# A hybrid RWKV-7 and block-sparse attention trunk on one core: g multiplied in split form, a fused key factor, openings to ScalarE, and a new order of work

## The chip, the cores and the metric

The kernel runs on one core of a Trainium2 chip. A core has TensorE (matrix products, results into PSUM banks), VectorE (DVE in the profile), ScalarE (ACT), GpSimd (POOL) and SyncE (SP), which issues the DMAs of this kernel. Each engine works through its own instructions in the order in which the program lists them, and waits on semaphores for the others. The metric is the device time of one execution in microseconds (us); lower is better.

## The reference, cut to what matters

Two layers over 256 tokens of width 1024, in float32: an RWKV-7 time mixing, and an attention layer. The sequence of 256 is one block of the block-sparse attention, so the second layer is plain causal attention of 16 heads of 64.

```python
def rwkv7_time_mix(h, ...):                      # h = rms_norm(x)
    xx = shifted(h) - h
    r, wdn, k, v, adn, gp = [(h + xx * mu[i]) @ w_in[:, cols(i)] for i in range(6)]
    decay = exp(-exp(-softplus(-(w0 + tanh(wdn) @ w2)) - 0.5))
    a = sigmoid(a0 + adn @ a2)
    kk = normalised_per_head(k * k_k)
    k = k * (1.0 + (a - 1.0) * k_a)
    # per token: S = S*decay - (S kk) (kk*a) + v k ;  y = S r
    y = group_norm(y) * gn_w + gn_b + sum(r * k * r_k) * v
    return (y * silu(gp)) @ w_out

x = x + rwkv7_time_mix(rms_norm(x))
kb, vb = shared_kv(x)                            # rms_norm, w_kv, norm and rotary on k
x = x + (softmax(q k^T, causal) v * silu(gate)) @ w_out_b
```

## The kernel before

**Projections.** x is held as two row blocks of 128 tokens (`b`) and the width as 8 k-tiles of 128. Each projection of the first layer is made in two halves of 512 columns (`n`): k0, r0, r1, k1, v0, v1, g0, g1, in the order `ORDER_A`. A half needs four quarters of its weights, each of 256 rows (two k-tiles) by 512 columns and 512 KB, which `loads` (L462) fetches into one of three `raw` buffers. Its other operand is the mixed input z = h + xx * mu, transposed, made by `mixed_split` (L684) into one or two of four pairs `zhi`, `zlo`.

A product of float32 operands is made in one of two ways in `products` (L501). *Split*: weights and z are each parted into a rounded high part (ScalarE copy into the type fp32r) and a low rest (VectorE subtraction, `split`, L381); three fp32r passes, low by high, high by low and high by high, go into the same PSUM bank. *Whole*: one float32 product of the unsplit operands, which the profile records as two rows. `WHOLE` lists the projections that are made whole: v and g. The split quarters lie in three pairs `whi`, `wlo`. A whole quarter stays in its `raw` buffer until both row blocks have used it.

**Recurrence.** The delta rule is computed in four chunks of 64 tokens. For each half n of the heads: `forms` (L855) makes the scaled keys, `in_chunks` transposes them and makes the products within a chunk (T, G), `inverse` (L972) inverts triangular blocks with many small VectorE steps and 32-wide TensorE products, and `recurrence` (L1122) runs chunk after chunk: TensorE, a copy by VectorE, TensorE, a scaling by ScalarE and VectorE, TensorE, a multiplication by VectorE. `evac_v` (L1068) centres v over each head of 64 and puts it into the operands `UV`. `group_norm` follows each row block, then `dense2` the output projection, whose second half of k-tiles needs the group norm of n = 1.

**Second layer.** Eight halves in the order `ORDER_B`; k, q, v and the gate g with inputs split in the same way; then scores, softmax, values, and the last output projection.

**What sets the order.** The program isn't written down in the order in which it runs. `Weave` simulates the engines while the program is being made: each part of the work is a generator that yields its operations with a rank from `PR` (lower goes first), and `dispatch` gives each free engine the ready operation with the lowest rank, by estimated durations. The order that comes out is fixed then; on the chip each engine follows it. Projection products have rank 100, so TensorE takes them when nothing else is ready. `either(a, b)` and `vg` leave an operation open to two engines. The second is taken only where the first one's backlog is longer by `ALT`:

```python
if op.alt and o is op.alt and self.backlog(op, prio) + op.us < o.us + ALT:
    continue
```

`Weave` also keeps a model of TensorE's clock (`COLD`, `WINDOW`, `PHASE`, `BUSY`, `KEEP`), and `warm_up` puts products of zeros before the first real ones until the planner's time `WARM[1]`. Buffers (`zs`, `his`, `raws`, `u2`, `bank`, `accs`) are given out by the same simulation.

Nearly all VectorE, ScalarE and GpSimd operations are recorded at L259, matrix products at L354, transposes at L357, DMAs at L364, whichever part they belong to; so groups are told apart by the tile names.

Of the kernel before, what the change touches and what calls it, by code (L numbers as in the profile page):

```python
# [37 lines left out]
class Op:  # L38
# [3 lines left out]
    def __init__(self, eng, us, emit, alt=None, table=None, columns=0.0, banks=(), port=0.0):  # L42
        self.eng, self.us, self.emit, self.alt, self.table = eng, us, emit, alt, table
        self.columns, self.banks, self.port = columns, banks, port
# [34 lines left out]
class Weave:  # L79
# [4 lines left out]
    def __init__(self):  # L84
        self.now, self.seq, self.heap = 0.0, 0, []
        self.queue = {e: [] for e in ("PE", "V", "S", "G", "D")}
        self.until = dict.fromkeys(self.queue, 0.0)
        self.table, self.parts, self.banks, self.recent = None, 0, {}, deque()
        self.port, self.holder = {"V": 0.0, "G": 0.0}, "V"
        self.window, self.active, self.cold = PHASE, 0.0, True  # L90
# [76 lines left out]
    def dispatch(self):  # L167
        for eng in ("PE", *("GV" if self.holder == "V" else "VG"), "S", "D"):
            queue = self.queue[eng]
            while self.until[eng] <= self.now + 1e-9:  # L170
                best, cooling = None, eng == "PE" and self.cooling()
                for entry in queue:
                    prio, seq, ready, o, op, _ = entry
                    if ready > self.now + 1e-9 or any(self.others(eng, b) > self.now + 1e-9 for b in o.banks):
                        continue
                    if o.port and self.port["G" if eng == "V" else "V"] > self.now + 1e-9:
                        continue
                    if op.alt and o is op.alt and self.backlog(op, prio) + op.us < o.us + ALT:
                        continue
                    key = (prio + (SWITCH if o.table not in (None, self.table) else 0)  # L180
                           - (1000 if cooling and o.columns > 2000 * o.us else 0), seq)
                    if best is None or key < best[0]:
                        best = key, entry
# [25 lines left out]
    def array(self, op):  # L209
# [4 lines left out]
        us, left = 0.0, 1.0  # L214
# [89 lines left out]
def yoco(ctx, tc, consts, x, norm_a, mu_a, w_in_a, w0_a, w2_a, a0_a, a2_a, kk_a, ka_a, rk_a,  # L304
# [43 lines left out]
    def pe(*mms):  # L348

        return Op("PE", sum(m[0] for m in mms), lambda: [m[1]() for m in mms], columns=sum(m[2] for m in mms),  # L350
                  banks=set().union(*(m[3] for m in mms)))

    def mm(dst, l, r, us, **kw):
        return us, lambda: nc.tensor.matmul(dst, l, r, **kw), size(r) * (1 if l.dtype == F32R else 4) * l.shape[0] / P, banks(dst)  # L354

    def tr(dst, src, idt):
        return max(0.045, 0.1085 * src.shape[0] / P), lambda: nc.tensor.transpose(dst, src, idt), 256 * src.shape[0] / P, banks(dst)  # L357
# [8 lines left out]
    def either(a, b):  # L366
        a.alt = b
        return a

# [250 lines left out]
    def normed(b, q, r):  # L620
# [4 lines left out]
        yield V.tensor_scalar(xn, xb[q, b], r, None, op0=ALU.mult)  # L625
        pt = yield bank
        yield tr4(pt, xn)
        if q == 0:
            yield V.tensor_tensor(hT[q][:, :, b1], pt.rearrange("p (a t) -> p a t", t=P), bc(na_T[:, 0:4], P), op=ALU.mult)
        else:  # L630
            yield [S.activation(hT[q][:, i, b1], pt[:, i * P:(i + 1) * P], AF.Copy, scale=na_T[:, 4 + i:5 + i])
                   for i in range(4)]
# [187 lines left out]
    def prep_k(n):  # L820
        yield event(f"ka{n}")
        for b in range(NB):
# [4 lines left out]
            yield vg("tensor_scalar", f, ia[n, b], 1.0, None, op0=ALU.subtract)  # L827
            yield vg("tensor_tensor", f, f, kab[f"ka{n}"], op=ALU.mult)
# [26 lines left out]
    def forms(n, b):  # L855
# [6 lines left out]
        yield V.tensor_scalar(nrm, nrm, 1e-24, None, op0=ALU.max)  # L862
# [109 lines left out]
    def inverse(n):  # L972
# [36 lines left out]
        yield V.tensor_scalar(XF[:, :, 0:16], X, w_th[0], None, op0=ALU.mult)  # L1009
        yield V.tensor_scalar(XF[:, :, 16:32], X, w_th[1], None, op0=ALU.mult)  # L1010
# [57 lines left out]
    def evac_v(n):  # L1068
        def f(b, acc):
# [10 lines left out]
            yield V.tensor_scalar(mv, mv, -1.0 / 64, None, op0=ALU.mult)  # L1080
            m4 = mv.rearrange("p (j q) -> p j q", q=2).unsqueeze(3).to_broadcast([P, 4, 2, 64])
            for cc in range(2):
                rows = slice(cc * 64, cc * 64 + 64)
                yield [vg("tensor_tensor", uv[n, 2 * b + cc][64 - q * 64:128 - q * 64, q], v4(vt)[rows, :, q, :],
                          m4[rows, :, q, :], op=ALU.add) for q in range(2)]
# [474 lines left out]
    for n in range(2):  # L1560
# [12 lines left out]
LAT, SWITCH, ALT = 0.16, 0, 24.59  # L1573
OWN = {"PE": 0.0, "V": 0.13, "S": 0.115, "G": 0.096, "D": 0.0}

PR = {"raw1": 55.8, "raw2": 76.3, "w2x": 32.2, "first": -129.5, "k0": 58.9, "r0": 111.3, "k1": -127.3, "r1": -14,
# [5 lines left out]
      "soft": 88.3, "values": -76.2, "out": 43.6}  # L1582

ORDER_A = ("k0", "r0", "r1", "k1", "v0", "v1", "g0", "g1")
FIRST = [(0, 1), (0, 0), (1, 1), (2, 1), (1, 0), (2, 0), (3, 0), (3, 1)]
# [3 lines left out]
WHOLE = "vg"  # L1589
ORDER_B = ("v0", "q1", "k0", "q0", "g1", "k1", "g0", "v1")  # L1590
# [4 lines left out]
COLD, WINDOW, KEEP, WARM = 1.9, 3.4133, 1852, (1.1, 5.39)  # L1595
PHASE, BUSY = 3.31, (3200, 3200)

# [53 lines left out]
```

## Time and profile before

| | us |
|---|---|
| median of 3 runs | 363.77 |
| lowest and highest | 363.22, 366.38 |
| the profiled execution | 362.5 |
| its span, first to last instruction | 360.7 |

The three runs took 366.38, 363.77 and 363.22. The profile is that of one execution; its mean granted TensorE clock is 0.991 of full speed. In the profile, a busy digit is the busy share of one of 40 equal slices in tenths. A group's row reads: line, engine, operation, out<-in by tile names, shape, count, then busy us and mean ns of one, then the idle time of the engine just before it and what ended it. In the timeline a row has the start, the duration and the number of equal instructions that were merged into it. Matrix products are pipelined, so that durations overlap: their pace is read from one start to the next.

### The profile page before, as it was taken

The numbers are of one execution on the slowest core, as the hardware profiler recorded it, in microseconds if no ns is written. First come the engines' busy times: TensorE is split into PE (matmuls) and PEld (weight loads), VectorE is DVE, ScalarE is ACT, GpSimd is POOL, SyncE is SP. The second block draws the span as 40 slices with busy tenths as digits, with TensorE's granted clock in tenths as the row PEclk, the third lists the DMA queues.
The fourth block names the chain that finished last, engine by engine and source line by source line (L and its number), as shares of the span: only waits on it lengthen the run. The fifth ranks groups of instructions, "written<-read, shape, count | busy, mean of one in ns | idle before, by whom it ended". The sixth has DMA issues, their size and how long they took to land.

```text
span 360.7 us, 7464 instructions
## 1 busy us (share of the span) xinstructions
PE 347.2 (96%) x2946; PEld 253.3 (70%) x2946; DVE 293.7 (81%) x588; ACT 187.6 (52%) x366; POOL 48.7 (14%) x73
## 2 busy tenths in 40 slices
PE   6999999999997999989999999999999999999995
PEld 5965668776554555465557777788889879876784
DVE  3999897999998689977759989658587879888653
ACT  5488948441061231242355357554664777698630
POOL 1100140000400000110102431005253005000000
PEclk9899999999999999998999999999999999999999
DMA  7764485454632724231544462475555353334303
GB/s 201 245 222 144 118 259 167 129 146 147 186 110 89 197 66 116 62 92 19 219 134 160 129 228 67 142 232 200 177 178 175 118 175 119 118 120 159 128 3 116
DMA packets 30331, 52.40 MB, mean 145 GB/s; under 512 B 4492, under 2 KB 5844, under 8 KB 30296
## 3 DMA queue, kind: packets, MB, share of 16 engines
q1 hardware_dynamic: 30296, 51.93, 46.5%
q8 instruction: 23, 0.38, 0.4%
q14 instruction: 12, 0.10, 0.1%
HBM read 48.26 MB, written 1.05 MB: 137 GB/s over the span
## 4 chain that ended last, share of the span: by engine, by line
PE 68%; DVE 15%; DMA 6%; ACT 5%; issue 3%; SPq 2%; POOL 0%; DVEq 0%; ACTq 0%
PE acc L354 51%; PE ps L354 12%; PE ps L357 5%; DVE UV L259 2%; DVE wlo L259 2%; ACT whi L259 2%; DVE u L259 2%; SPq L364 2%; DMA tri<-in_consts_dram 2%; DMA raw<-in_w_in_a_dram 2%; DMA raw<-in_w_kv_dram 1%; DVE XF L259 1%; DMA x<-in_x_dram 1%; DVE zlo L259 1%; DVE vn L259 1%
## 5 line engine op out<-in xcount | busy, mean ns | idle before, releaser
L259 DVE TENSOR_TENSOR wlo<-raw,whi 128x1024 fp32r<-128x1024 f32 x62 | 75.5, 1221 | 24.3 <-ACT whi L259 24.1
L259 ACT ACTIVATE whi<-raw 128x1024 fp32r<-128x1024 f32 x62 | 65.4, 1059 | 47.2 <-PE acc L354 30.2
L354 PE MATMUL acc<-whi,z 128*128 128x512 f32 x128 | 39.7, 392 | 0.0
L354 PE MATMUL acc<-wlo,zhi 128*128 128x512 f32 x88 | 37.9, 431 | 0.9 <-DVE wlo L259 0.7
L354 PE MATMUL acc<-whi,zlo 128*128 128x512 f32 x88 | 34.6, 393 | 0.0
L354 PE MATMUL acc<-whi,zhi 128*128 128x512 f32 x88 | 34.5, 393 | 0.0
L354 PE MATMUL acc<-raw,zhi 128*128 128x512 f32 x64 | 32.8, 637 | 0.0
L354 PE MATMUL acc<-raw,zlo 128*128 128x512 f32 x64 | 32.0, 617 | 0.0
L354 PEld LDWEIGHTS acc<-whi,z 128*128 128x128 f32 x128 | 24.1, 188 | 4.8
L354 PE MATMUL acc<-wlo,z 128*128 128x512 f32 x64 | 26.1, 408 | 0.0
L354 PE MATMUL acc<-zb,whi 128*128 128x256 f32 x128 | 23.1, 281 | 0.0
L354 PEld LDWEIGHTS acc<-wlo,zhi 128*128 128x128 f32 x88 | 16.5, 188 | 6.3 <-DVE wlo L259 2.4
L354 PE MATMUL acc<-whi,zb 128*128 128x512 f32 x64 | 20.0, 394 | 0.0
L354 PE MATMUL acc<-whi,zf 128*128 128x512 f32 x64 | 19.8, 391 | 0.0
L354 PEld LDWEIGHTS acc<-zb,whi 128*128 128x128 f32 x128 | 19.6, 188 | 0.0
L354 PEld LDWEIGHTS acc<-whi,zhi 128*128 128x128 f32 x88 | 16.5, 188 | 3.7
L354 PEld LDWEIGHTS acc<-whi,zlo 128*128 128x128 f32 x88 | 16.6, 188 | 3.3 <-issue 0.5
L354 PE MATMUL acc<-zb,wlo 128*128 128x256 f32 x64 | 18.9, 295 | 0.0
L259 ACT ACTIVATE UV<-ps 64x256 f32<-64x256 f32 x8 | 3.0, 378 | 29.6 <-DVE UV L259 16.3
L259 POOL TENSOR_TENSOR nrm<-nrm,half 128x8 f32<-128x8 f32 x4 | 7.8, 1950 | 77.5 <-DVE nrm L259 77.5
L354 PEld LDWEIGHTS acc<-raw,zhi 128*128 128x128 f32 x64 | 11.5, 197 | 9.4 <-issue 8.7
L354 PEld LDWEIGHTS acc<-raw,zlo 128*128 128x128 f32 x64 | 10.8, 189 | 9.4 <-issue 8.4
(216 smaller groups left out, 727.2 us busy)
## 6 DMA issues: line engine op xcount, KB each, us to landing
raw<-in_w_in_a_dram SPq DMA_DIRECT2D x32, 512.0 KB
raw<-in_w_kv_dram SPq DMA_DIRECT2D x16, 512.0 KB
raw<-in_w_in_b_dram SPq DMA_DIRECT2D x16, 512.0 KB
raw<-in_w_out_a_dram SPq DMA_DIRECT2D x8, 512.0 KB
raw<-in_w_out_b_dram SPq DMA_DIRECT2D x8, 512.0 KB
x<-in_x_dram SPq DMA_DIRECT2D x8, 256.0 KB
out_dram<-x SPq DMA_DIRECT2D x8, 128.0 KB
sw<-eL SPq DMA_DIRECT2D x8, 126.0 KB
```

Source lines behind the costliest of these rows:

```text
L259: return Op(eng, us, lambda: getattr(obj, name)(*a, **k), table=table, banks=banks(*a, *k.values()), port=port(eng, name, us, a, k))
L354: return us, lambda: nc.tensor.matmul(dst, l, r, **kw), size(r) * (1 if l.dtype == F32R else 4) * l.shape[0] / P, banks(dst)
L357: return max(0.045, 0.1085 * src.shape[0] / P), lambda: nc.tensor.transpose(dst, src, idt), 256 * src.shape[0] / P, banks(dst)
L364: return Op("D", us, lambda: [nc.sync.dma_start(a, b) for a, b in pairs])
```

## The change

1. `WHOLE` goes from "vg" to "v". g is made in the split form: its z goes through `split`, in two pairs `zhi`, `zlo` where one did, and its eight weight quarters are split by ScalarE and VectorE into `whi`, `wlo`.
2. In `prep_k` the two steps (ia − 1), times k_a, become one fused VectorE instruction.
3. Several operations that were VectorE's alone get ScalarE as an alternative through `either`: the normalised input and its gain for q = 0 (`normed`), two scalings in `inverse`, the scaling of the mean and the centring of v in `evac_v` (as four ScalarE activations, made into one operation by the new `several`). The `max` of the key norm gets GpSimd as an alternative; the centring loses it.
4. The planner learns of small TensorE operations: `narrow` marks those with fewer than 128 rows or columns; a change between narrow and full costs `SWAP` = 0.1 us in its simulation, and an operation of the other kind ranks later by `STICK` = 19.2.
5. All ranks in `PR` and several constants are new, and so are the order of the second layer's projections and the last two entries of `FIRST`. Warm-up products run until 8.23 of the planner's time rather than 5.39.

```diff
-    def __init__(self, eng, us, emit, alt=None, table=None, columns=0.0, banks=(), port=0.0):
+    def __init__(self, eng, us, emit, alt=None, table=None, columns=0.0, banks=(), port=0.0, narrow=False):
...
-                    key = (prio + (SWITCH if o.table not in (None, self.table) else 0)
+                    key = (prio + (SWITCH if o.table not in (None, self.table) else STICK if eng == "PE" and o.narrow != self.narrow else 0)
...
-        us, left = 0.0, 1.0
+        us, left = 0.0 if op.narrow == self.narrow else SWAP, 1.0
+        self.narrow = op.narrow
...
+    def several(ops):
+
+        return Op(ops[0].eng, sum(o.us for o in ops), lambda: [o.emit() for o in ops], banks=set().union(*(o.banks for o in ops)),
+                  port=sum(o.port for o in ops))
...
-        yield V.tensor_scalar(xn, xb[q, b], r, None, op0=ALU.mult)
+        yield either(V.tensor_scalar(xn, xb[q, b], r, None, op0=ALU.mult), S.activation(xn, xb[q, b], AF.Copy, scale=r))
...
-            yield vg("tensor_scalar", f, ia[n, b], 1.0, None, op0=ALU.subtract)
-            yield vg("tensor_tensor", f, f, kab[f"ka{n}"], op=ALU.mult)
+            yield V.scalar_tensor_tensor(f, ia[n, b], -1.0, kab[f"ka{n}"], op0=ALU.add, op1=ALU.mult)
...
-        yield V.tensor_scalar(nrm, nrm, 1e-24, None, op0=ALU.max)
+        yield vg("tensor_scalar", nrm, nrm, 1e-24, None, op0=ALU.max)
...
-        yield V.tensor_scalar(XF[:, :, 0:16], X, w_th[0], None, op0=ALU.mult)
-        yield V.tensor_scalar(XF[:, :, 16:32], X, w_th[1], None, op0=ALU.mult)
+        yield [either(V.tensor_scalar(XF[:, :, i * 16:i * 16 + 16], X, w_th[i], None, op0=ALU.mult),
+                      S.activation(XF[:, :, i * 16:i * 16 + 16], X, AF.Copy, scale=w_th[i])) for i in range(2)]
...
-                yield [vg("tensor_tensor", uv[n, 2 * b + cc][64 - q * 64:128 - q * 64, q], v4(vt)[rows, :, q, :],
-                          m4[rows, :, q, :], op=ALU.add) for q in range(2)]
+                dst = [uv[n, 2 * b + cc][64 - q * 64:128 - q * 64, q] for q in range(2)]
+                yield [either(V.tensor_tensor(dst[q], v4(vt)[rows, :, q, :], m4[rows, :, q, :], op=ALU.add),
+                              several([S.activation(dst[q][:, j, :], v4(vt)[rows, j, q, :], AF.Identity,
+                                                    bias=mv[rows, 2 * j + q:2 * j + q + 1]) for j in range(4)]))
+                       for q in range(2)]
...
-LAT, SWITCH, ALT = 0.16, 0, 24.59
+LAT, SWITCH, ALT = 0.16, 1.0, 26.61
...
-FIRST = [(0, 1), (0, 0), (1, 1), (2, 1), (1, 0), (2, 0), (3, 0), (3, 1)]
+FIRST = [(0, 1), (0, 0), (1, 1), (2, 1), (1, 0), (2, 0), (3, 1), (3, 0)]
...
-WHOLE = "vg"
-ORDER_B = ("v0", "q1", "k0", "q0", "g1", "k1", "g0", "v1")
+WHOLE = "v"
+ORDER_B = ("q0", "q1", "v0", "k0", "g1", "k1", "g0", "v1")
...
-COLD, WINDOW, KEEP, WARM = 1.9, 3.4133, 1852, (1.1, 5.39)
+COLD, WINDOW, KEEP, WARM = 1.9, 3.4133, 1045, (1.1, 8.23)
...
+SWAP, STICK = 0.1, 19.2
```

Of the ranks, those that the text names: `w` (weight splits from the fifth quarter on) goes from 82.4 to 58.2, `rec0` and `rec1` from −130 and 0.3 to 29.4 and −23.9, `inv0` and `inv1` from −77.8 and −83.1 to −69.4 and −78.7, `zg` from −65.2 to 77.6.

More of the change, by code (lines that the diff above doesn't have):

```diff
@@ L38 @@
 class Op:
-    def __init__(self, eng, us, emit, alt=None, table=None, columns=0.0, banks=(), port=0.0):
+    def __init__(self, eng, us, emit, alt=None, table=None, columns=0.0, banks=(), port=0.0, narrow=False):
         self.eng, self.us, self.emit, self.alt, self.table = eng, us, emit, alt, table
-        self.columns, self.banks, self.port = columns, banks, port
+        self.columns, self.banks, self.port, self.narrow = columns, banks, port, narrow
 class Slots:
@@ L89, in __init__ @@
         self.port, self.holder = {"V": 0.0, "G": 0.0}, "V"
-        self.window, self.active, self.cold = PHASE, 0.0, True
+        self.window, self.active, self.cold, self.narrow = PHASE, 0.0, True, False
     def at(self, t, f):
@@ L350, in pe @@
         return Op("PE", sum(m[0] for m in mms), lambda: [m[1]() for m in mms], columns=sum(m[2] for m in mms),
-                  banks=set().union(*(m[3] for m in mms)))
+                  banks=set().union(*(m[3] for m in mms)), narrow=any(m[4] for m in mms))
     def mm(dst, l, r, us, **kw):
-        return us, lambda: nc.tensor.matmul(dst, l, r, **kw), size(r) * (1 if l.dtype == F32R else 4) * l.shape[0] / P, banks(dst)
+        return us, lambda: nc.tensor.matmul(dst, l, r, **kw), size(r) * (1 if l.dtype == F32R else 4) * l.shape[0] / P, banks(dst), min(l.shape[0], size(l)) < P
     def tr(dst, src, idt):
-        return max(0.045, 0.1085 * src.shape[0] / P), lambda: nc.tensor.transpose(dst, src, idt), 256 * src.shape[0] / P, banks(dst)
+        return max(0.045, 0.1085 * src.shape[0] / P), lambda: nc.tensor.transpose(dst, src, idt), 256 * src.shape[0] / P, banks(dst), src.shape[0] < P
     def tr4(pt, src):
@@ L628, in normed @@
         if q == 0:
-            yield V.tensor_tensor(hT[q][:, :, b1], pt.rearrange("p (a t) -> p a t", t=P), bc(na_T[:, 0:4], P), op=ALU.mult)
+            yield either(V.tensor_tensor(hT[q][:, :, b1], pt.rearrange("p (a t) -> p a t", t=P), bc(na_T[:, 0:4], P), op=ALU.mult),
+                         several([S.activation(hT[q][:, i, b1], pt[:, i * P:(i + 1) * P], AF.Copy, scale=na_T[:, i:i + 1])
+                                  for i in range(4)]))
         else:
@@ L1079, in f @@
             yield V.tensor_reduce(out=mv, in_=heads(vt), op=ALU.add, axis=AX.X)
-            yield V.tensor_scalar(mv, mv, -1.0 / 64, None, op0=ALU.mult)
+            yield either(V.tensor_scalar(mv, mv, -1.0 / 64, None, op0=ALU.mult), S.activation(mv, mv, AF.Copy, scale=-1.0 / 64))
             m4 = mv.rearrange("p (j q) -> p j q", q=2).unsqueeze(3).to_broadcast([P, 4, 2, 64])
@@ L1569, in yoco @@
     weave.run()
-LAT, SWITCH, ALT = 0.16, 0, 24.59
+LAT, SWITCH, ALT = 0.16, 1.0, 26.61
 OWN = {"PE": 0.0, "V": 0.13, "S": 0.115, "G": 0.096, "D": 0.0}
-PR = {"raw1": 55.8, "raw2": 76.3, "w2x": 32.2, "first": -129.5, "k0": 58.9, "r0": 111.3, "k1": -127.3, "r1": -14,
[5 rows of a table removed]
-      "soft": 88.3, "values": -76.2, "out": 43.6}
+PR = {"raw1": 78.4, "raw2": 2.3, "w2x": 63.5, "first": -69.4, "k0": 122.5, "r0": 101.8, "k1": 90.1, "r1": 33.6,
[5 rows of a table added]
+      "values": 50.6, "out": -114.3}
 ORDER_A = ("k0", "r0", "r1", "k1", "v0", "v1", "g0", "g1")
-FIRST = [(0, 1), (0, 0), (1, 1), (2, 1), (1, 0), (2, 0), (3, 0), (3, 1)]
+FIRST = [(0, 1), (0, 0), (1, 1), (2, 1), (1, 0), (2, 0), (3, 1), (3, 0)]
 FIRST_B = [(0, 0), (1, 0), (2, 0), (0, 1), (1, 1), (2, 1), (3, 1), (3, 0)]
 SINGLE = "k"
-WHOLE = "vg"
-ORDER_B = ("v0", "q1", "k0", "q0", "g1", "k1", "g0", "v1")
+WHOLE = "v"
+ORDER_B = ("q0", "q1", "v0", "k0", "g1", "k1", "g0", "v1")
 N_U2, N_RAW = 4, 3
 URGENT = (1, 0)
-COLD, WINDOW, KEEP, WARM = 1.9, 3.4133, 1852, (1.1, 5.39)
+COLD, WINDOW, KEEP, WARM = 1.9, 3.4133, 1045, (1.1, 8.23)
 PHASE, BUSY = 3.31, (3200, 3200)
+SWAP, STICK = 0.1, 19.2
 def _constants():
```

10 rows, old and new, of the table PR are left out of this document.

## The prediction, made before the changed kernel was run

> **What bounds the kernel now.** I read the page first: the span, the engine totals, the slices of DVE and TensorE, and the shares of the chain that ended last.
>
> ```profile
> span 360.7 us, 7464 instructions
> PE 347.2 (96%) x2946; PEld 253.3 (70%) x2946; DVE 293.7 (81%) x588; ACT 187.6 (52%) x366; POOL 48.7 (14%) x73
> PE   6999999999997999989999999999999999999995
> DVE  3999897999998689977759989658587879888653
> PE 68%; DVE 15%; DMA 6%; ACT 5%; issue 3%; SPq 2%; POOL 0%; DVEq 0%; ACTq 0%
> ```
>
> TensorE is busy 96% of the span and carries 68% of the chain; no slice after the first shows it below 7 tenths, but for the last. VectorE is the second resource: nine tenths in a dozen slices, and 15% of the chain. ScalarE has half of its time free. So work taken from TensorE can shorten the kernel, but only where VectorE does not step into its place. The table by stage says where that could be. Columns: stretch, its length, busy time of TensorE, weight loads, VectorE, ScalarE and GpSimd, then the granted clock, DMA share and GB/s.
>
> ```profile
> 9.40:13.00 3.60, 3.60 (x18) 3.60 (x19) 3.60 (x8) 1.48 (x2) 0.84 (x3) 0.54 0.81 268
> 20.00:40.00 20.00, 19.89 (x69) 12.48 (x69) 17.94 (x35) 17.92 (x29) 0.00 (x0) 1.00 0.47 149
> 40.00:60.00 20.00, 18.37 (x112) 13.85 (x113) 18.50 (x32) 14.91 (x37) 4.90 (x4) 1.00 0.66 197
> 84.00:204.00 120.00, 116.19 (x1647) 68.94 (x1646) 101.76 (x206) 39.25 (x83) 12.62 (x14) 0.99 0.41 121
> 162.80:166.40 3.60, 3.60 (x8) 1.13 (x4) 3.47 (x6) 0.38 (x1) 0.00 (x0) 0.53 0.00 0
> ```
>
> From 84 to 204 us the two inverses, the two recurrences and the v and g projections run together. VectorE has 120 − 101.8 = 18.2 us free there, ScalarE 80.
>
> **The change, part by part.** The sum is made against the profiled execution, 362.5 us (span 360.7); the median of the runs is 363.8, and I carry the difference over at the end.
>
> *g split instead of whole (TensorE).* The four rows stand around the border between the last split projection and the first whole one.
>
> ```profile
> 84.09 0.39 PE L354 MATMUL acc<-wlo,zhi 128*128 128x512 f32 x1
> 85.45 0.39 PE L354 MATMUL acc<-wlo,zhi 128*128 128x512 f32 x1
> ...
> 86.81 7.03 PE L354 MATMUL acc<-raw,zhi 128*128 128x512 f32 x16
> 93.68 0.59 PE L354 MATMUL acc<-raw,zlo 128*128 128x512 f32 x1
> ```
>
> Six split passes go from 84.09 to 85.45, 0.227 us each from start to start, so a product of three passes takes 0.68. Sixteen rows of the whole form go from 86.81 to 93.68, 0.429 each, and a product is two rows, 0.86. (The 0.39 and 0.59 in the rows are durations with the pipelined tail; starts are what counts.) g has 2 halves × 2 row blocks × 8 k-tiles = 32 products: 32 × 0.86 = 27.5 becomes 32 × 0.68 = 21.8. **Term: −5.7**, all on the bounding engine.
>
> *g split instead of whole (VectorE, ScalarE).* Eight weight quarters and four z pieces must now be split.
>
> ```profile
> L259 DVE TENSOR_TENSOR wlo<-raw,whi 128x1024 fp32r<-128x1024 f32 x62 | 75.5, 1221 | 24.3 <-ACT whi L259 24.1
> L259 DVE TENSOR_TENSOR zlo<-u,zhi 128x512 fp32r<-128x512 f32 x4 | 2.7, 686 | 0.1
> L259 DVE TENSOR_SCALAR k<-ia 128x512 f32<-128x512 f32 x4 | 1.7, 422 | 0.1
> L259 DVE SCALAR_TENSOR_TENSOR k<-k,acc 128x512 f32<-128x512 f32 x4 | 2.7, 676 | 0.0
> L259 ACT ACTIVATE whi<-raw 128x1024 fp32r<-128x1024 f32 x62 | 65.4, 1059 | 47.2 <-PE acc L354 30.2 <-DMA raw<-in_w_in_a_dram 5.4 <-DMA raw<-in_w_out_a_dram 4.3
> L259 ACT ACTIVATE zhi<-u 128x512 fp32r<-128x512 f32 x4 | 2.5, 623 | 0.0
> ```
>
> VectorE gains 8 × 1.22 + 4 × 0.69 = 12.5 us, ScalarE 8 × 1.06 + 4 × 0.62 = 11.0. Both fit into the 18.2 and 80 us free, VectorE's with 5.7 to spare. No DMA is added: the eight quarters are fetched by the same SyncE issues, and a raw buffer now comes free after its split, not after its products. What this costs TensorE is a wait for a late `wlo`. The nearest rows are the 20 to 60 us stage, where sixteen quarters are split for k and r with VectorE as busy: TensorE idled 40 − 38.3 = 1.7 us there in all, 0.11 a quarter. Eight quarters: **+0.9**; bounds 0 (all hidden) and 12.5 (none).
>
> *One step of the key factor.* Four subtractions of 0.42 go; the multiply that stays takes the fused form, 0.68 as in the row of k from acc, as long as before. VectorE −1.7, at about 28 to 36 us, where TensorE loses 0.1 us in 20: hidden, **0**, bounds −1.7 and 0. The `max` of the norm stays on VectorE unless its queue is long; 0.
>
> *Openings to ScalarE.* The planner takes an alternative only where the backlog of the first engine exceeds the alternative by ALT (24.59, now 26.61 us), a queue that rows of half a microsecond hardly build. The rows bear it out: operations that already had an alternative never used it.
>
> ```profile
> L259 DVE COPY Z<-ZX 32x512 f32<-32x512 f32 x8 | 3.3, 417 | 0.1
> L259 DVE TENSOR_SCALAR bv<-bv,rsum 128x256 f32<-128x256 f32 x12 | 4.2, 347 | 0.0
> L259 DVE TENSOR_TENSOR UV<-vn,mv 64x256 f32<-64x256 f32 x16 | 6.7, 420 | 0.3
> L259 DVE TENSOR_SCALAR XF<-xw,con 128x256 f32<-128x256 f32 x4 | 1.3, 350 | 0.0
> L259 DVE TENSOR_SCALAR xn<-x,rs 128x512 f32<-128x512 f32 x4 | 1.8, 482 | 0.0
> ```
>
> All 8 spreads of Z ran on VectorE with ScalarE open to them, and so did the softmax scalings. So the centring of v (16, 6.7 us), the scalings of XF and xn (1.3, 1.8) stay where they are: **0**, with −9.8 of VectorE time as the bound if they all go.
>
> *Longer warm-up (5.39 to 8.23).* It adds dummy matmuls ahead of the first low-rank products.
>
> ```profile
> 9.38 3.61 PE L354 MATMUL ps<-hT,wl 128*128 128x128 f32 x16 [1.65 <-DMA wl<-in_w_in_a_dram]
> 12.83 0.60 PE L357 MATMUL ps<-con,xn 128*128 128x128 f32 x4
> ...
> 16.49 1.06 PE L354 MATMUL ps<-hT,wl 128*128 128x128 f32 x8
> 17.39 1.95 PE L354 MATMUL ps<-xxT,wm 128*128 128x128 f32 x16
> ```
>
> The first 16 took 3.45 us at a granted clock of 0.54 (first row of the table by stage); eight of the same later took 0.90, so 16 take 1.8. TensorE idled 1.65 us before them; dummies there would keep the clock. Up to −1.7. VectorE was busy in all 3.6 us of that stretch, so part comes back as waits for `xxT` and z: **−1.0**, bounds −1.7 and 0. Beside it: the Trainium skill, "TensorE: Matmul & The Clock Gate", Part 1, has the clock halve after an idle window of about 3.4 us and return after a busy one. The trace agrees with the halving and its length (3.6 us at 0.54). By that rule alone this term would be the full −1.7.
>
> *The end of the recurrence.* The second half of the output projection needs the group norm that follows the last chunk. Last `zlo` of each row block, and the first product that reads it:
>
> ```profile
> 202.85 0.69 DVE L259 TENSOR_TENSOR zlo<-ps,zhi 128x512 fp32r<-128x512 f32 x1
> 210.05 0.68 DVE L259 TENSOR_TENSOR zlo<-ps,zhi 128x512 fp32r<-128x512 f32 x1
> ...
> 206.68 0.39 PE L354 MATMUL acc<-zlo,zhi 128*128 128x512 f32 x1
> 213.28 0.40 PE L354 MATMUL acc<-zlo,zhi 128*128 128x512 f32 x1
> ```
>
> Ready at 203.5 and 210.7, read at 206.7 and 213.3: a slack of 3.1 and 2.6 us. A cover that shrinks by 5.7 against a chain that does not move exposes 5.7 − 2.6 = 3.1 us of idle TensorE. The chain does move: its steps wait behind products of 0.68 in place of 0.86, and with less cover it waits for less. Between 0 and 3.1 I take **+1.4**, near the middle.
>
> *The new order.* Labels and buffers change everywhere. Among the later projections only the first four change places; attention half 0 still has all four behind it, half 1 its keys after the sixth and its values after the eighth. g takes two z pairs, not one, and the second comes free only when k is through; that is well ahead of g. FIRST exchanges its last two entries. What another order does to the half-speed stretch at 162.8 (3.6 us at 0.53, 1.7 us lost) is open: **0**, bounds −1.7 and +1.7.
>
> Sum: −5.7 + 0.9 − 1.0 + 1.4 = −4.4, 362.5 to 358.1; on the median 363.8 to **359.4**.
>
> **The rivals.**
>
> *The chain holds.* If inverse and recurrence keep their length and the front gives nothing, only the slack is won: 363.8 − 2.6 = 361.2. For it: the chain is a ping-pong between engines, and 12.5 us more VectorE work stand beside it. Against: TensorE had hardly an idle slice there, so the chain was waiting for TensorE too.
>
> *VectorE's new work lands on the chain (slower).* Its place is 112 to 204 us. A subtraction of 1.22 us, once begun, is not interrupted, and every copy, scaling and multiply of inverse and recurrence that becomes ready meanwhile stands behind it; TensorE then runs dry before the group norm. If all eight stand in the chain it ends 9.8 us later; less the slack of 2.6 and the front's 1.0 that is +6.2: 370. It makes the kernel slower by over 3.6 us once more than 7.2 us, six of the eight, are met. For it: after the change VectorE would hold about 114 of 120 us. Against: the weight splits have a late rank (58.2) against the chain's (29.4, −23.9, −69.4, −78.7).
>
> *Fewer switches between small and full matmuls.* The planner now charges 0.1 us for one.
>
> ```profile
> 106.84 1.29 PE L354 MATMUL ps<-ZX,AB 16*32 16x32 f32 x128
> ...
> 126.12 1.98 PE L354 MATMUL acc<-raw,zlo 128*128 128x512 f32 x4
> 128.03 1.14 PE L354 MATMUL ps<-ZX,QS 32*32 32x32 f32 x60
> ...
> 199.33 0.69 PE L354 MATMUL ps<-UV,RR 128*64 128x64 f32 x16
> ```
>
> Four whole rows between two small blocks hold TensorE from 126.12 to 128.03, 1.91 where 4 × 0.429 = 1.72 would do: 0.19 a visit. From 106.84 to 199.33 I count 32 visits in the timeline. Half of them joined would give −3.0: 356.4. Against: a small part already ranks before every projection product (rank 100) with 19.2 added, so the new rule moves only small parts against transposes. Beside it: the Trainium skill, "TensorEngine Tiling (Array Packing)", Key Properties, says that a change of tiling mode drains the array; the trace agrees, with these 0.19 us.
>
> *ScalarE takes its openings after all.* VectorE then gains only 12.5 − 1.7 − 9.8 = 1.0 us, and the terms +0.9 and +1.4 go: 363.8 − 6.7 = 357.1.
>
> **How the numbers follow.** The forecast 0.38, switches 0.07, openings 0.05, the chain holds 0.30, VectorE slower 0.20. The runs shown lie within 363.2 to 366.4, so about 1% (3.6 us) is what a measurement can tell from no change. Faster by over 1% are the forecast and the two that go further, 0.50; within 1% the held chain, 0.30; slower 0.20. Likeliest 359.4, its own range 357 to 360. The wider range goes down past the joined switches with the full front and the half-speed stretch gone (356.4 − 0.7 − 1.7 = 354) and up to 368, inside the slower case: about one in ten left out on either side.
>
> **What would show it.** Right: half as many whole products (`raw`) as before, `wlo` 70 and no idle of TensorE over 1 us between 112 and 210; centring and XF still on VectorE; hT·wl 16 rows in about 1.8 us; the second-half products of the output projection start 4 to 6 us earlier than 206.7. The held chain: those products at 203 to 205 behind an idle TensorE. The slower case: VectorE above 9 tenths from 112 to 204, TensorE waiting for `wlo`, `u` or `UV`, and a granted clock below 1.0 in those stretches. What would make the sum wrong is above all the +1.4, taken between its bounds without a row that shows it.

## The result, and the profile after

| | before | after |
|---|---|---|
| median | 365.38 us (363.22 to 367.88, 20 runs) | 361.49 us (357.71 to 365.17, 20 runs) |
| ratio after to before | | 0.985, 95% interval 0.982 to 0.988 |
| profiled execution | 362.5 us, span 360.7, granted clock 0.991 | 362.5 us, span 360.7, granted clock 0.980 |

The ratio leaves out seven of the changed kernel's 20 runs, those more than 1.5% slower than its fastest; over all runs the medians stand at 0.989. The kernel is faster by 1.5%, or by 1.1% between the medians. The time lies inside the range and 2.1 us above the predicted 359.4. Of these 2.1 us, 1.6 come from the base: the forecast went from 363.8, the median of three runs, and 20 runs of the same kernel give 365.38. The change itself is −3.9 us between the medians, where the sum had −4.4. The two profiled executions happen to take the same time, and yet they are not the same: where one won, the other lost again.

The page of the changed kernel, engine totals, three rows of the slices, the shares of the chain:

```profile
PE 345.5 (96%) x2988; PEld 264.4 (73%) x2988; DVE 303.0 (84%) x596; ACT 201.0 (56%) x380; POOL 47.0 (13%) x73
PE   7999999999989999889999999999999999999995
DVE  2999889999999899997689989787457789999743
PEclk9999999999999999996599999999999999999999
PE 65%; DVE 26%; DMA 3%; issue 3%; ACT 2%; SPq 1%; POOL 0%; DVEq 0%; ACTq 0%
```

VectorE has 9.3 us more work than before, and its share of the chain went from 15% to 26%. The row of the granted clock dips to 6 and 5 tenths in two slices, near 170 us. The groups of instructions:

```profile
L355 PE MATMUL acc<-raw,zhi 128*128 128x512 f32 x32 | 14.9, 599 | 0.0
L355 PE MATMUL acc<-raw,zlo 128*128 128x512 f32 x32 | 14.9, 602 | 0.0
L260 DVE TENSOR_TENSOR wlo<-raw,whi 128x1024 fp32r<-128x1024 f32 x70 | 85.3, 1222 | 22.9 <-ACT whi L260 22.7
L260 DVE TENSOR_TENSOR UV<-vn,mv 64x256 f32<-64x256 f32 x16 | 6.7, 419 | 0.3
L260 DVE TENSOR_SCALAR xn<-x,rs 128x512 f32<-128x512 f32 x4 | 1.8, 483 | 0.0
L260 DVE SCALAR_TENSOR_TENSOR k<-ia,bv 128x512 f32<-128x512 f32 x4 | 2.8, 688 | 0.0
```

Half as many whole products, eight more low parts, the fused step in four instructions. All sixteen additions that centre v and the scalings of xn are still on VectorE: the openings to ScalarE were not used. Three places of the timeline: the first low-rank products, the first whole product, and the first product of the output projection's second half.

```profile
9.37 2.02 PE L355 MATMUL ps<-hT,wl 128*128 128x128 f32 x16 [0.62 <-DVE xxT L260]
...
85.76 6.60 PE L355 MATMUL acc<-raw,zhi 128*128 128x512 f32 x15
...
208.40 0.39 PE L355 MATMUL acc<-zlo,zhi 128*128 128x512 f32 x1
```

They were at 86.81 and 206.68 before. The front is 1.05 us shorter; but the middle took 122.64 us where it had taken 119.87, and only the second layer (152.3 us to the end, from 154.0) brings the total back. What TensorE waited for between 84 and 205 us (engine, line, releaser: us in total, times, longest):

```profile
PE ps L355 <- DVE UV L260: 1.8, 2, 1.0
PE ps L358 <- DVE sw L260: 1.4, 1, 1.4
PE ps L355 <- DVE u L260: 0.6, 1, 0.6
```

VectorE is named in all three. (The one for `sw` ends at 101 us, before the recurrence.) The longest of the first row is found in VectorE's timeline. The scaled operand `UV` is made in two halves, and between them stands a product of the second half's inverse, 1.00 us long:

```profile
149.48 0.42 DVE L260 TENSOR_TENSOR UV<-ps,eLT 64x256 f32<-64x256 f32 x1
149.82 1.00 DVE L260 TENSOR_TENSOR tmp<-xw 128x512 f32<-128x512 f32 x1
150.85 0.43 DVE L260 TENSOR_TENSOR UV<-ps,eLT 64x256 f32<-64x256 f32 x1
```

TensorE began its products at 150.04 and stood still for 0.99 us until the second half was there:

```profile
150.04 0.30 PE L355 MATMUL ps<-UV,WL 128*64 128x64 f32 x2
151.33 0.68 PE L355 MATMUL ps<-UV,WL 128*64 128x64 f32 x14 [0.99 <-DVE UV L260]
```

Then comes the loss. The table by stretches (columns as in the prediction) for the 15 us of such spells and the 14 us after them:

```profile
150.00:165.00 15.00, 11.46 (x371) 8.78 (x371) 14.13 (x24) 4.81 (x8) 3.66 (x3) 1.00 0.07 21
165.00:179.00 14.00, 14.00 (x213) 11.03 (x208) 9.21 (x16) 4.60 (x8) 0.00 (x0) 0.51 0.29 83
```

TensorE was busy for 11.5 of 15 us (13.5 before), and then ran 14 us at a granted clock of 0.51. It looks fully busy there because everything takes twice as long. The half-speed stretch of before was 3.6 us at 0.53.

### The profile page after: what moved, and what is told of

Read it like the earlier page. It is cut to its first block, busy times and chain, and to the rows that moved or that the text cites. A ratio compares the mean times of both kernels' runs of the same rounds, so it can differ in the third digit from the quotient of the medians.

```text
span 360.7 us, 7573 instructions
## 1 busy us (share of the span) xinstructions
PE 345.5 (96%) x2988; PEld 264.4 (73%) x2988; DVE 303.0 (84%) x596; ACT 201.0 (56%) x380; POOL 47.0 (13%) x73
## 3 DMA queue, kind: packets, MB, share of 16 engines
HBM read 48.26 MB, written 1.05 MB: 137 GB/s over the span
## 4 chain that ended last, share of the span: by engine, by line
PE 65%; DVE 26%; DMA 3%; issue 3%; ACT 2%; SPq 1%; POOL 0%; DVEq 0%; ACTq 0%
PE acc L355 45%; PE ps L355 15%; PE ps L358 5%; DVE wlo L260 4%; DVE XF L260 3%; DVE u L260 3%; DMA sw<-eL 2%; DVE tmp L260 2%; DVE UV L260 2%; DVE zlo L260 2%; DVE xw L260 1%; DVE RR L260 1%; DVE k L260 1%; DVE WL L260 1%; DMA vrow<-in_mu_a_dram 1%
## 5 line engine op out<-in xcount | busy, mean ns | idle before, releaser
L260 DVE TENSOR_TENSOR wlo<-raw,whi 128x1024 fp32r<-128x1024 f32 x70 | 85.3, 1222 | 22.9 <-ACT whi L260 22.7
L260 ACT ACTIVATE whi<-raw 128x1024 fp32r<-128x1024 f32 x70 | 74.0, 1060 | 46.0 <-PE acc L355 37.1
L355 PE MATMUL acc<-wlo,zhi 128*128 128x512 f32 x120 | 53.1, 442 | 0.5 <-ACT zhi L260 0.4
L355 PE MATMUL acc<-whi,zlo 128*128 128x512 f32 x120 | 47.9, 399 | 0.2 <-DVE zlo L260 0.2
L355 PE MATMUL acc<-whi,zhi 128*128 128x512 f32 x120 | 47.8, 398 | 0.0
L355 PEld LDWEIGHTS acc<-whi,zhi 128*128 128x128 f32 x120 | 23.0, 192 | 5.3
L260 ACT ACTIVATE zhi<-u 128x256 fp32r<-128x256 f32 (+1 forms) x16 | 8.2, 531 | 12.6 <-DVE u L260 12.6
L355 PE MATMUL acc<-raw,zhi 128*128 128x512 f32 x32 | 14.9, 599 | 0.0
L355 PE MATMUL acc<-raw,zlo 128*128 128x512 f32 x32 | 14.9, 602 | 0.0
L355 PEld LDWEIGHTS acc<-wlo,z 128*128 128x128 f32 x64 | 12.0, 188 | 2.8 <-issue 0.5
```

Of the source, the lines that this page charges most:

```text
L260: return Op(eng, us, lambda: getattr(obj, name)(*a, **k), table=table, banks=banks(*a, *k.values()), port=port(eng, name, us, a, k))
```

## The experiments

"Middle" is the stretch from the first whole product to the output projection's first second-half product, in the one profiled execution of each; the clock is the range over all its runs.

| run | median us (runs) | ratio to before, 95% | middle us | granted clock |
|---|---|---|---|---|
| changed, second sample | 358.54 (4) | 0.984, 0.972 to 0.996 | 119.30 | 0.980 to 1.000 |
| changed, g whole | 367.54 (10) | 1.002, 0.997 to 1.008 | 121.41 | 0.980 to 1.000 |
| before, g split | 380.74 (4) | 1.045, 1.033 to 1.057 | 131.03 | 0.958 to 0.967 |
| g's low parts on ScalarE | 358.60 (4) | 0.981, 0.961 to 1.000 | 117.32 | 0.979 to 1.000 |
| g's low parts made twice | 369.26 (10) | 1.009, 1.005 to 1.012 | 129.96 | 0.976 to 1.000 |
| g's low parts on GpSimd | 366.86 (10) | 0.998, 0.994 to 1.001 | 126.75 | 0.966 to 0.986 |
| warm-up of ten products | 360.26 (4) | 0.985, 0.980 to 0.991 | 118.80 | 0.967 to 1.000 |
| zero passes in the gaps | 359.32 (6) | 0.979, 0.976 to 0.981 | 120.10 | 0.995 to 1.000 |
| key factor in two steps | 359.58 (4) | 0.982, 0.978 to 0.986 | 118.85 | 0.993 to 1.000 |
| second half's v centred by ScalarE | 356.92 (4) | 0.974, 0.970 to 0.978 | 115.25 | 0.995 to 1.000 |
| the same, order of the change | 360.75 (6) | 0.986, 0.980 to 0.992 | 120.48 | 0.976 to 0.999 |
| all v centred by ScalarE | 360.19 (4) | 0.982, 0.977 to 0.987 | 115.67 | 0.995 to 1.000 |

**The changed kernel once more.** No edit.

> The changed kernel unaltered, for a second profile. Theory A (the clock): the shorter products leave TensorE idle spells between 149 and 164 us, and in some executions its clock then falls to half for up to four stretches; time and granted clock go together, about 0.36 us for each 0.001 of mean clock, from 356 us of span at 1.000. Then this profile lies on that line, and the less clock it lost between 160 and 180 us, the shorter it is by half of the time lost. Theory B (the chain): the time is set by the recurrence whatever the clock; then two profiles with different clocks have the same span within 1 us.

Its profiled execution kept full clock: 359.1 us, span 357.3. The same two stretches and the same landmarks:

```profile
150.00:165.00 15.00, 11.08 (x359) 8.35 (x359) 13.87 (x23) 4.98 (x8) 3.67 (x3) 1.00 0.06 20
165.00:179.00 14.00, 13.24 (x279) 9.97 (x279) 12.88 (x21) 6.03 (x10) 1.84 (x2) 1.00 0.36 116
```

```profile
85.74 6.60 PE L355 MATMUL acc<-raw,zhi 128*128 128x512 f32 x15
...
205.04 0.39 PE L355 MATMUL acc<-zlo,zhi 128*128 128x512 f32 x1
```

279 matrix products in 165 to 179 us where the other execution made 213: the 3.4 us between the two (208.40 − 205.04) are the clock. The idle spells before are the same in both, so they do not bring the fall each time. Over all 24 runs of the changed kernel the nine with a clock of 0.999 or above take 358.4 us on average, the four at 0.980 take 362.9 and the four at 0.971 take 364.1. (The kernel before is no steadier: in the 54 runs of it that were made beside the experiments its clock lies between 0.976 and 0.995, 0.987 on average, and the changed kernel's average is 0.988.)

**Split of g alone, both ways.**

```diff
-WHOLE = "v"
+WHOLE = "vg"    # in the changed kernel; the reverse in the kernel before
```

> The changed kernel with g multiplied whole again, all else kept. It takes 5.7 us back onto TensorE and 12.5 us off VectorE. If the split of g is nearly the whole gain: ratio to the kernel before 0.995 to 1.003 (the warm-up's 1 us is what stays). If the new order, warm-up and fused step bring it: 0.985 to 0.990, as the full change.

> The kernel before with the one edit that g is split, ranks and all else kept. If the split carries the gain by itself: ratio 0.985 to 0.993. If it needs the new order, because VectorE's 12.5 us otherwise land on the chain: 0.997 to 1.02.

The changed kernel with g whole, at full clock in its profile (0.999):

```profile
85.58 6.60 PE L355 MATMUL acc<-raw,zhi 128*128 128x512 f32 x15
...
206.99 0.39 PE L355 MATMUL acc<-zlo,zhi 128*128 128x512 f32 x1
```

With g whole the new order is no faster than before (1.002); with g split it is. At a clock of 0.999 or more the two runs with g whole take 364.0 us on average and the nine with g split 358.4, so that the split is worth 5.6 us there, about the 5.7 that TensorE saves. In the two profiles it is 4.3 us of the span: the middle is 121.41 − 119.30 = 2.1 us shorter, and the time from its end to the end of the kernel 2.3 (154.6 and 152.3 us).

In the order planned for the kernel before, the same split makes it 4.5% slower. TensorE's longest wait there, and the stretch around it:

```profile
PE ps L357 <- DVE yn L259: 6.2, 2, 5.9
180.00:200.00 20.00, 16.13 (x391) 12.80 (x393) 18.52 (x30) 5.62 (x7) 1.35 (x2) 0.57 0.33 108
```

From 177.94 to 183.87 us TensorE waits for `yn`, which a group norm of the first half has to finish, while VectorE is busy with that group norm, with steps of the second half's inverse and with one weight subtraction. That subtraction, at 180.17, belongs to the output projection: the eight of g run from 125.43 to 168.57. From 180.94 to 198.00 the clock is at half. The middle is 11.2 us longer than before, and the stages in front of it and behind it 5.0 us each. So this is the kind of wait that the prediction's slower rival described, VectorE holding up the chain, but not the rival as it was priced, by g's eight subtractions alone. Both variants are planned anew, so that "the same edit" comes with another order in each, and how much of the 4.5% is the order's is not shown.

**VectorE's subtractions off, twice, and on GpSimd.** TensorE's order is that of the changed kernel in all three.

```diff
-        yield from split(raw, hi, lo)
+        yield S.activation(hi, raw, AF.Copy)
+        o = V.tensor_tensor(lo, raw, hi.bitcast(F32), op=ALU.subtract)
+        if i in of_g:                     # the eight quarters of g
+            o.emit = lambda: nc.scalar.activation(lo, raw, AF.Copy)
+            # or: two VectorE subtractions; or nc.gpsimd.tensor_tensor(...)
+        yield o
```

> The changed kernel, the same order on TensorE; the low parts of g's eight weight quarters are written by a ScalarE copy of the weights where VectorE subtracted (the subtraction is left out, so g's low part is not the reference's). It takes 9.8 us off VectorE between 112 and 200 us. If VectorE feeds the idle spells of TensorE at 149 to 164 us: their 4 us shrink below 2, the half-speed stretch with them, ratio to the kernel before about 0.975. If VectorE's new work is hidden: ratio 0.985, as the full change.

> The changed kernel with each of g's eight low-part subtractions run twice on VectorE (the second writes the same values): 8 x 1.22 = 9.8 us more of VectorE's time between 85 and 205 us, TensorE's order unchanged. Writing them on ScalarE saved 2.0 us of that stretch (119.3 to 117.3). If VectorE's queue is part of the chain there with its full weight, the stretch from the first whole product to the first product of the second half grows by 5 to 10 us (124 to 129) and the time is 364 to 368 us at full clock. If the eight subtractions lie mostly beside other work, as the prediction took it (0.9 of 9.8 us), the stretch grows by 0.5 to 3 us and the time is 359 to 362 us at full clock.

> The changed kernel with g's eight low-part subtractions on GpSimd instead of VectorE; the values are the same, TensorE's order unchanged. If only VectorE's load matters, the stretch from the first whole product to the first product of the second half falls by about 2 us, as it did with ScalarE (119.3 to 117.3), and the time is 356 to 357 us at full clock. Rival: a 128x512 subtraction takes GpSimd several times VectorE's 1.22 us, so that the low parts come late and TensorE waits for them: 1 to 8 us longer, with TensorE's idle time ended by GpSimd's wlo.

9.8 us less on VectorE win 2.0 us in the middle of the one profile; between runs at a clock of 0.998 or more it is 0.6 us (357.7 and 358.4), less than such runs differ among themselves, so that 2.0 is the most that can be put down to them. 9.8 us more lengthen it by 10.7 (129.96 − 119.30), the clock's fall in that profile included (0.989). Between runs at a clock of 1.000 it is 10.0: 369.06 and 367.73 us against 358.4. TensorE's waits with the subtractions made twice:

```profile
PE ps L355 <- DVE u L260: 4.6, 4, 1.6
PE ps L355 <- DVE UV L260: 4.0, 5, 1.4
```

So the changed kernel stands at the edge: VectorE's queue is nearly full, the first 9.8 us fit but for at most 2.0, and of the next 9.8 nothing fits. GpSimd is no way out. It takes 2.4 us for each, and it also stops some of VectorE's instructions, as these rows of GpSimd, then of VectorE, show:

```profile
139.54 2.38 POOL L499 TENSOR_TENSOR wlo<-raw,whi 128x1024 fp32r<-128x1024 f32 x1 [2.35 <-ACT whi L260]
143.10 2.39 POOL L499 TENSOR_TENSOR wlo<-raw,whi 128x1024 fp32r<-128x1024 f32 x1 [1.18 <-ACT whi L260]
...
157.25 5.17 POOL L499 TENSOR_TENSOR wlo<-raw,whi 128x1024 fp32r<-128x1024 f32 x2
```

```profile
139.63 2.31 DVE L260 TENSOR_TENSOR tmp<-xw 128x8 f32<-128x8 f32 x1
143.27 2.49 DVE L260 TENSOR_TENSOR UV<-vn,mv 64x256 f32<-64x256 f32 x1
...
157.35 2.85 DVE L260 TENSOR_TENSOR vn<-vn,bon 128x512 f32<-128x512 f32 x1
160.13 1.04 DVE L260 STREAM_TRANSPOSE ZX<-XF 128x512 f32<-128x512 f32 x1
```

A product of 128x8, 0.16 us in the changed kernel, took 2.31, an addition that centres v, 0.41 there, took 2.49, and the multiplication of vn, 0.67 there, took 2.85, each while GpSimd subtracted. The transpose in the last row, beside the next subtraction, kept its length (1.05 in the changed kernel). TensorE's longest idle spell in this run, 3.0 us, ends with the `UV` that stood behind the last of the three. No wait of TensorE ends with GpSimd's `wlo`, as the rival had it: the loss comes by way of VectorE, and by a clock of 0.966 to 0.986 in all ten runs.

**The warm-up cut back to ten products.** Nothing else moves.

```diff
+            o = pe(mm(t[:, 0:P], z, z, 0.2155, start=True, stop=True))
+            count[0] += 1
+            if count[0] > 10:
+                o.emit = lambda: None
+            yield o
```

> The changed kernel with only the first ten of its fifteen zero products at the start, the count of the kernel before; everything else in its place. If the longer warm-up is what keeps TensorE at full clock through the first real products, the sixteen hT by wl products at about 9 us go back from 2.0 us to about 3.4 us, the first product of the whole multiplication starts about 1.0 us later (86.7 to 86.9 instead of 85.7), and the time is about 1.0 us above the unaltered changed kernel in executions of the same clock. Rival: the gain of the front comes from the new order and the zero products have no part in it; then the first product stays within 0.3 us of 85.7.

```profile
9.63 3.75 PE L355 MATMUL ps<-hT,wl 128*128 128x128 f32 x16 [1.82 <-DVE u L260]
```

3.75 us in place of 2.02, and the clock is at 0.50 from 9 to 13 us. The first whole product comes at 87.13. In the six profiles of the changed kernel and its variants with the long warm-up and an unchanged front it comes between 84.85 and 86.30 (85.71 on average), so the loss is 0.8 to 2.3 us. Not all of it is the clock: two runs of this kernel at 1.000 took 360.0 and 360.2 us, still 1.7 and 1.9 above the changed kernel's 358.4 at that clock.

**Zero passes in the idle spells.** 24 extra passes with a zero operand among g's products.

```diff
+BALLAST = {18: 5, 19: 5, 22: 5, 23: 3, 24: 3, 25: 3}     # g's product number: passes
+                more = [mm(acc, z(0, kt), zeros, 0.0, start=False, stop=False) for _ in range(extra)]
+                o.emit = lambda: [m[1]() for m in parts[:2] + more + parts[2:]]
```

> The changed kernel with 24 extra passes of zeros (each as wide as a pass of g's product, about 0.23 us, 5.5 us in all) put among the products of g at the six places ahead of TensorE's idle spells between 100 and 164 us; the output is the same. Theory A, idle TensorE makes the clock fall in 160 to 180 us: the passes fill the idle, the half-speed stretch goes from the profile, and the times gather at 357 to 361 us, with the granted clock at 0.99 or above in nearly all runs. Theory B, the clock falls for a reason that the idle spells have no part in: the granted clock and the spread of the times (357 to 365 us) stay as they are, and the passes cost what of their 5.5 us does not fit into the idle spells, 0 to 4 us on top. Theory C, the spells are too short to hold the passes and VectorE's chain sets the time: 2 to 5 us longer at equal clock.

```profile
150.00:165.00 15.00, 14.64 (x296) 11.47 (x298) 14.65 (x26) 6.13 (x9) 3.64 (x3) 1.00 0.09 21
165.00:179.00 14.00, 13.81 (x350) 10.97 (x347) 12.11 (x22) 5.58 (x10) 1.59 (x2) 1.00 0.30 99
```

Useless work for 5.5 us cost 0.8 us in the middle, and the six runs lie at 0.995 to 1.000. Theory A holds. The ratio to before, 0.979 (0.976 to 0.981), is even lower than that of the change, 0.985 (0.982 to 0.988). In the three kernels whose spells are filled or fewer (this one and the two below whose order was planned for another centring), all 14 runs have a clock of 0.995 or more; in the six that keep the spells (the two samples of the change, the low parts on ScalarE, the short warm-up, the unfused factor, the centring moved in the old order) 14 of 42 are below 0.985. Where one spell is longer, low clocks are commoner: 9 of 10 with the low parts on GpSimd (a spell of 3.0 us), 4 of 4 in the kernel before with g split (5.9 us).

**The openings, forced.** The centring of v for the second half, then for both, given to ScalarE, each with a new order; then for the second half with every instruction in the changed kernel's order.

```diff
-                yield [either(V.tensor_tensor(dst[q], ...), several([S.activation(dst[q][:, j, :], ...) ...]))
+                yield [several([S.activation(dst[q][:, j, :], ...) ...]) if n else V.tensor_tensor(dst[q], ...)
```

> The changed kernel with the centring of v for the second half (8 additions of 0.42 us on VectorE) forced onto ScalarE, as the opening in the change would allow: 8 times four activations of a 64x64 block, about 1 us each time (64x128 takes ScalarE 0.26 us, 64x256 takes 0.38 us). The planner makes a new order. Those additions stand among VectorE's queue between 143 and 149 us. If VectorE's load in 140 to 160 us is what makes TensorE wait, 3.4 us less of it shorten the stretch from the first whole product to the second half's first product by 0.5 to 2 us, and the idle spells at 151 to 164 us shrink: 356 to 358 us at full clock. Rival: the chain of the second half's inverse sets those spells and ScalarE's four activations come later than VectorE's one: the same to 3 us slower.

> The changed kernel with all sixteen additions that centre v forced onto ScalarE: 6.7 us off VectorE, about 16 us on ScalarE, whose busy share is 56%; the planner makes a new order. The prediction's bound for this opening: it would help by what VectorE's work stands on the chain. If each us off VectorE in the recurrence is worth what the eight subtractions were (2.0 us of 9.8), 1.4 us shorter: about 357 us at full clock. Rival: ScalarE then delays its own high parts (whi, 1.06 us each) and the chain, and the time is 1 to 5 us longer, which would be why the openings were left unused.

> The changed kernel with the same eight additions that centre v for the second half given to ScalarE as before (8 times four activations of 0.33 us), but with every other instruction in the order of the changed kernel. It tells whether that version's 356.9 us came from VectorE's queue (3.4 us shorter between 143 and 149 us) or from the new order that was planned with it. If from the queue: TensorE's idle spells at 151 to 164 us (0.99, 0.63, 0.85, 1.15 us) shrink to half or less, the stretch from the first whole product to the second half's first product falls from 119.3 to about 116 to 118 us, the granted clock stays at 0.99 or above, and the time is 355.5 to 357.5 us. If from the new order: spells, stretch and the clock's spread stay as in the changed kernel, 358 to 362 us.

The first is faster than both kernels: 356.92 us, ratio 0.974 (0.970 to 0.978) where the change has 0.985 (0.982 to 0.988).

```profile
150.00:165.00 15.00, 14.00 (x458) 10.95 (x457) 14.75 (x26) 9.80 (x27) 2.73 (x3) 1.00 0.17 56
165.00:179.00 14.00, 13.42 (x200) 10.07 (x200) 13.46 (x22) 7.56 (x14) 2.21 (x2) 1.00 0.58 190
```

TensorE is busy for 14.0 us in place of 11.1 to 11.5. The middle is 4.1 us shorter than in the second sample and the front 0.9 (84.88 against 85.74); 1.6 of it is given back before the end (span 354.0 against 357.3). With everything in the old order, though, 3.4 us less on VectorE brought nothing (360.75). VectorE's timeline of that run shows why:

```profile
144.77 0.24 DVE L260 TENSOR_TENSOR tmp<-xw 128x50 f32<-128x50 f32 x1
146.88 0.43 DVE L260 TENSOR_SCALAR UV<-ps 64x256 f32<-64x256 f32 x1 [1.87 <-ACT UV L260]
```

Behind the activations, of which four take ScalarE 1.07 us (12 in 3.22) where VectorE took 0.42, VectorE now stands still for 1.87 us, and TensorE idles at nearly the same places as before (0.91, 0.69 and 0.84 us). So less load on VectorE does not give the gain by itself; the first version has it together with its new order. Whether that order would give it with the centring left on VectorE was not run. With all sixteen moved the middle is as short (115.67), but TensorE then waits on the last block's output (0.8 us for x, 0.7 for zhi) and the time is 360.19.

**The key factor unfused.**

```diff
-            yield V.scalar_tensor_tensor(f, ia[n, b], -1.0, kab[...], op0=ALU.add, op1=ALU.mult)
+            o.emit = lambda: [nc.vector.tensor_scalar(f, ia[n, b], 1.0, None, op0=ALU.subtract),
+                              nc.vector.tensor_tensor(f, f, kab[...], op=ALU.mult)]
```

> The changed kernel with the key factor's fused step given back as two VectorE instructions in the same place (4 more VectorE instructions), everything else in its order. The prediction's term is 0, with 1.7 us as the bound. If that term is right the time stays within 1 us of the unaltered changed kernel at equal clock (357.1 to 359.9 at full clock), and the first whole product stays within 0.5 us of 85.7. Rival: the four instructions lie on the chain that leads to the recurrence, and the second half's first product comes 1 to 2 us later than 205.0.

The first whole product came at 86.48, 0.7 us later, and the three runs at full clock took 359.7 us on average, 1.4 above the changed kernel's. The front of kernels that are equal there varies by 1.45 us (84.85 to 86.30), more than that difference, so this is not settled: the fusion is worth between 0 and about 1.4 us.

## Why the prediction was right, and where its terms were off

The direction was right, and so was what the sum rests on: TensorE bounds the kernel, and g's split is worth 5.6 us of the time in runs at full clock. That the total came near is in part luck, because the stages did not give what the sum had in them. The table is in us; it sets the second sample of the change, at full clock, beside the profile of before (0.991), whose middle holds a half-speed stretch worth up to 1.7:

| stage | before | change | difference | predicted |
|---|---|---|---|---|
| to the first whole product | 86.81 | 85.74 | −1.07 | −1.0 |
| from there to the second half's first product | 119.87 | 119.30 | −0.57 | −5.7 + 0.9 + 1.4 = −3.4 |
| from there to the end | 154.02 | 152.28 | −1.74 | 0 |
| span | 360.70 | 357.32 | −3.38 | −4.4 |

The middle gave a sixth of its forecast, and the second layer gave 1.7 us that no term had. The prediction's own signs came in part. Half the whole products, `wlo` 70, the unused openings, the warm first products and no idle spell over 1 us (0.99; 1.15 in the second profile) are there. But the second-half products of the output projection start at 208.40 and 205.04, not 4 to 6 us before 206.7; 205.04 is just past the 203 to 205 that was to be the sign of the held chain.

- **g split, TensorE, −5.7.** The products went as counted: 64 whole rows became 32. Without the subtractions the split brings 121.41 − 117.32 = 4.1 us of the middle.
- **The end of the recurrence, +1.4.** The price was not paid where it was looked for. Most of the slack is still there: in the second profile the last `zlo` of the two row blocks are ready at 202.1 and 209.7 and read at 205.0 and 211.4, which leaves 3.0 and 1.7 us (3.1 and 2.6 before). TensorE idles earlier, for 3.9 of the 15 us from 150 to 165, where it idled 1.5.
- **VectorE's wait for `wlo`, +0.9.** Mis-sized, inside its bounds: the subtractions cost at most 2.0 us. The mechanism was another: none of TensorE's waits listed above is for `wlo`; it waits for `u` and `UV`, which stand behind other work in the queue. The rows from 20 to 60 us, from which the term was taken, have no such chain.
- **The slower rival** was put at six of eight subtractions met. With the planned order at most a fifth of their time is met (2.0 of 9.8 us); with the subtractions doubled all of the added time is. So the rival was a real one. That the order keeps it away is not shown: the kernel before with g split is slower, but with none of g's subtractions in its longest wait.
- **The new order, 0 within ±1.7.** With g whole the middle of the new order is 1.5 us longer than before (121.41 against 119.87, one profile each), which lies inside these bounds. What lies outside is the half-speed stretch, whose 1.7 us of one execution the prediction carried as the most that could come or go: in the profiled execution of the change it lasted 13.65 us, and over the runs the time moves with it by 5.7 us (358.4 to 364.1). The median is not where this shows, since the kernel before loses as much clock on average.
- **The second layer, −1.7**, was not in the sum at all. In the new order with g whole it took 154.6 us, so it is not the order by itself; what in the second layer's order brings it was not separated.
- **Warm-up, −1.0.** Right in size: 2.02 us for the sixteen products, and the cut-back version loses 0.8 to 2.3 us.
- **Key factor 0, openings 0.** The openings were inert, as read from the operations that already had them. The key factor is open between 0 and −1.4, inside its bounds.

## What to carry to other kernels

Before work is moved from the bounding engine to the second one, look at what stands behind that work in the second engine's queue: the price is in the chain's small instructions that wait there, not in the moved instructions themselves, and it rises steeply once that queue is full (at most 2.0 us for the first 9.8, 10.0 for the next). Freeing the queue helps only with an order that uses it, since an engine that waits in order for the new owner stands as still as a busy one. Where runs of one kernel spread, read the granted clock of each run first: one profile says little of a stage where the clock falls in some executions only.

## What the runs showed of the hardware

**The clock is lost in equal portions.** The edges of the half-speed stretch in the profile of the change:

```profile
165.00:165.50 0.50, 0.50 (x8) 0.35 (x3) 0.50 (x1) 0.00 (x0) 0.00 (x0) 0.83 0.00 0
178.50:179.00 0.50, 0.50 (x2) 0.40 (x3) 0.50 (x2) 0.00 (x0) 0.00 (x0) 0.52 0.85 328
```

A third of the first half microsecond and nearly all of the last are at half clock, so the stretch runs from 165.33 to 178.98: 13.65 us, four times 3.41. With the centring moved and the order kept:

```profile
161.50:162.00 0.50, 0.50 (x13) 0.38 (x7) 0.50 (x2) 0.33 (x1) 0.00 (x0) 0.52 0.19 45
168.00:168.50 0.50, 0.50 (x13) 0.50 (x14) 0.50 (x1) 0.44 (x1) 0.00 (x0) 0.65 0.00 0
```

From 161.52 to 168.35: 6.83, twice 3.41. The mean clocks of most runs lie near 1.000, 0.995, 0.990, 0.986, 0.981, 0.976 and 0.971, which are the same steps: 3.41 × 0.5 / 360 = 0.0047 for each portion. Some lie between two, as three of the 24 runs of the change do (0.993). A line through the 24 runs of the change gives 1.0 us of time for one. The Trainium skill, "TensorE: Matmul & The Clock Gate", Part 1, has a window of 3413 ns that runs freely and does not start with the kernel. The portions agree with it, and a window that lies differently in each execution would explain why the same idle spells cost the clock in some runs and not in others; that is argued, not shown. The page's table of the two states names an idle window as what brings half speed. Here TensorE was busy for 11.5 of the 15 us before the fall, with many 32-wide products among them, and no spell was longer than 1 us. So a window without any work was not needed; how much idleness is enough was not measured.

**GpSimd stops some of VectorE's instructions.** In the run with the low parts on GpSimd three VectorE instructions of 0.16, 0.41 and 0.67 us took 2.31, 2.49 and 2.85 us beside subtractions of 2.4 us. The Trainium skill, "SBUF — State Buffer", "SBUF: two separate sides", says that the two share one pair of ports, held for a whole instruction; the trace agrees for these three, which all combine two operands that lie in SBUF. It isn't so for every instruction beside a subtraction: a scaling of one operand took 0.72 us in place of 0.35 (at 136.63), and the transposes, reductions and reads of PSUM kept their length, as the 1.04 us of the transpose at 160.13 show.
